# Second attention of a two-block layer: values as the stationary operand, two groups side by side, three branches in one PSUM sum; two more places for expert weights

## Chip, cores, metric

One core of a Trainium2 chip runs the whole program as one launch. The metric is the device time of an execution in microseconds (us). Engines work in parallel, each through its own queue in a fixed order: TensorE (PE; its weight loads are PEld), VectorE (DVE), ScalarE (ACT), GpSimd (POOL) and SyncE (SP), which here issues nearly all weight loads.

## What is computed

Two transformer blocks on 256 tokens of width 1024, fp32 throughout. The first has a forgetting attention beside a convolution, a cross attention to a memory, and a hierarchical mixture of 32 experts. The second has an HGRN2 mixer beside a sparse attention, then a feed-forward part and a gated embedding. The change is in the sparse attention and in the places for expert weights. With 256 tokens the 16 selectable blocks and the window of 512 hold all causal keys, so "selected" and "window" are two causal attentions with keys and values of their own, over the same rotated queries:

```python
s = einsum('bgrqd,bgnd->bgrqn', qb, k_cmp); p_cmp = masked_softmax(s, cmp_end <= t)   # 15 compressed keys
o_cmp = einsum('bgrqn,bgnd->bgrqd', p_cmp, v_cmp)
o_sel = einsum('bgrqk,bgqkd->bgrqd', masked_softmax(qr @ kg, m_sel), vg)              # causal
o_win = einsum('bgrqk,bgkd->bgrqd', masked_softmax(qr @ kwb, m_win), vwb)             # causal
out = gt[:, :, 0] * o_cmp + gt[:, :, 1] * o_sel + gt[:, :, 2] * o_win                 # 16 heads, 4 groups g of 4 heads r, d = 64
merged = sigmoid(ga) * (y_a @ w_branch_a) + sigmoid(gb) * (y_b @ w_branch_b)          # y_b = out
```

## The kernel before

Dense products split fp32 into two fp32r parts (activations into h and l, weights into wh by ScalarE, L184, and wl by VectorE, L185) and add three products in PSUM. `dense_nat` takes 512 output columns at a time: 48 matmuls per call, two loads of 1 MB into the `ring` of four places, each split in two pieces. Instructions are put in order for each engine by a planner that simulates the program and takes, of what is ready, that with the highest priority; `high_priority(offset=n)` moves a part ahead by n instructions. Weight loads and splits are 1000 ahead, the second attention (`att`) is `ATT` = 1300 ahead of its place, so dense products fill in where attention isn't ready.

Expert weights come in loads of 1 MB (one expert's half matrix) into "places" that open as memory of the first block comes free: 8 (`NRB`) when the first attention is done, the four of the ring, 2 + 2 + 2 more, three pairs of the split buffers, and 1 (`NRD`) at the end of the cross attention. `mload` fills place after place in turn; the first 22 loads need nothing of the routing.

In the second block `nsa` makes compressed keys and values and the compressed branch (L1448 to L1480: P is turned, multiplied with the block-diagonal VB and copied into yb), then keys (kh, kl, both halves of the partitions hold a copy), values vt and rotated queries qr (one half of the partitions the h part, the other the l part). Then `att` runs head by head: scores of both branches at once (for queries 0 to 127 against 128 keys, for queries 128 to 255 against 256), the largest of each row by VectorE, exponentials with their sums by ScalarE, three transposes of P per branch, and P times V with P as the stationary operand and 64 columns of vt moving. For each pair of heads VectorE scales the sums out of PSUM and adds both branches to yb. Beside it run the rest of `gate("a")`, `gate("b")` and the product with w_branch_a. After it yb is turned by 16 transposes into the operand of w_branch_b. Tiles of 4 KB per partition (qr, kh, kl, yb, the second gate, ...) share 16 slots (`s4`).

Of the kernel before, what the change touches and what calls it, by code (L numbers as in the profile page):

```python
# [8 lines left out]
F32 = mybir.dt.float32  # L9
# [3 lines left out]
OP = mybir.AluOpType  # L13
# [4 lines left out]
D = 1024  # L18
# [11 lines left out]
NRB, NR2, NRC, NRE, NRD = 8, 2, 2, 2, 1  # L30
# [107 lines left out]
class B:  # L138
# [25 lines left out]
    def wload(self, ap, kc, n, ring=None):  # L164
# [25 lines left out]
    def wchunk(self, ap, kc, n, ring=None):  # L190
        with self.tc.high_priority(offset=self.ahead):
            return self.wsplit(self.wload(ap, kc, n, ring), kc, n)
# [4 lines left out]
    def dense_nat(self, xT, w, K, c0, n, evac, halves=2, ring=None):  # L197
# [4 lines left out]
        for kg in range(0, KC, 4):  # L202
            g = min(4, KC - kg)
            wh, wl = self.wchunk(w[kg * 128:(kg + g) * 128, c0:c0 + n], g, n, ring)
# [935 lines left out]
    def mixer(self, on):  # L1140
# [4 lines left out]
        with tc.tile_pool(name="sm2", bufs=1) as self.sm, tc.tile_pool(name="b2", bufs=1) as b2, \  # L1145
# [21 lines left out]
            with tc.tile_pool(name="hg", bufs=2) as hg:  # L1167
                yb, att = self.hgrn(uT, W, on, hv, hg, php, self.nsa(uT, W, s4, b2))
            self.tap("on", ya[0])
            first.close()  # L1170
            with tc.tile_pool(name="s5", bufs=2) as s5p, tc.tile_pool(name="ap", bufs=1) as ap, \
# [4 lines left out]
                with tc.high_priority(offset=ATT):  # L1176
                    att(ap, pax)
# [27 lines left out]
                self.tap("yb0", yb[0])  # L1205
                self.tap("yb1", yb[1])
                yT = self.tr_parts(yb, self.parts(s4p, tag="s4"))

# [7 lines left out]
                for c in range(2):  # L1216
                    self.dense_nat(yT, A["w_branch_b_2"], D, c * 512, 512, ev_m(c))
# [133 lines left out]
    def nsa(self, uT, W, s4, b2):  # L1351
# [15 lines left out]
        VB = b2.tile([64, 4, 64], F32, name="VB")  # L1367
        nc.gpsimd.memset(KB, 0.0)

        def compress():  # L1370
# [36 lines left out]
            for c in range(2):  # L1407
# [4 lines left out]
            V.tensor_tensor(VB, pk[:, 1, None, :].to_broadcast([64, 4, 64]),  # L1412
                            self.cst("blk")[:64, :, None].to_broadcast([64, 4, 64]), op=OP.mult)
# [32 lines left out]
        yb = [s4("yb") for _ in range(2)]  # L1446

        for hf in range(2):  # L1448
# [68 lines left out]
        def att(ap, pax):  # L1517

            acc, Ps, PTs = {}, {}, {}

            def scores(h):
                g, j = h // 4, h % 2
                if not j:
                    acc[h // 2] = (self.pat.tile([128, 2, 2, 2, 64], F32, name="po"),
                                   self.sm.tile([128, 2, 2, 2], F32, name="asm", bufs=3))
                sm = acc[h // 2][1]
                nm = self.sm.tile([128, 2, 2], F32, name="anm", bufs=2)
                P = Ps[h] = ap.tile([128, 2, 384], F32, name="P", bufs=2)  # L1530
                rr = slice(64 * j, 64 * j + 64)
                for hf, kb, c0 in ((0, 128, 0), (1, 256, 128)):
                    sc = self.ptr.tile([128, 2, kb], F32, name="tr")
                    q = qr[g][:, h % 4, hf * 128:(hf + 1) * 128]
                    self.mm(sc, q, kh[g // 2][:, g % 2, :, :kb], True, False)
                    self.mm(sc, q[rr], kl[g // 2][rr, g % 2, :, :kb], False, False)
                    self.mm(sc[:, :, kb - 128:], self.idr,
                            self.cnr[:, None, :].to_broadcast([128, 2, 128]), False, True)
                    self.exps(sc, P[:, :, c0:c0 + kb], kb, nm[:, hf, :], sm[:, hf, :, j])

            def turn(h):
                P = Ps.pop(h)
                PT = PTs[h] = ap.tile([128, 2, 384], F32, name="PT", bufs=2)
                for br in range(2):
                    pt = pax.tile([128, 384], F32, name="hp")
                    for b in range(3):
                        nc.tensor.transpose(pt[:, b * 128:(b + 1) * 128], P[:, br, b * 128:(b + 1) * 128], idn)  # L1547
                    (V.tensor_copy if br else nc.scalar.copy)(PT[:, br, :], pt)

            def values(h):  # L1550
                g, j = h // 4, h % 2
                po, sm = acc[h // 2]
                PT = PTs.pop(h)
                for br in range(2):
                    v = lambda m: vv[br][:, m, g * 64:(g + 1) * 64]
                    self.mm(po[:, 0, br, j, :], PT[:, br, 0:128], v(0), True, True)
                    self.mm(po[:, 1, br, j, :], PT[:, br, 128:256], v(0), True, False)
                    self.mm(po[:, 1, br, j, :], PT[:, br, 256:384], v(1), False, True)
                if not j:
                    return  # L1560
                rc = self.sm.tile([128, 2, 2, 2], F32, name="arc", bufs=2)
                V.reciprocal(rc, sm)
                V.tensor_tensor(rc, rc, gn[:, :, 1:3, h - 1:h + 1], op=OP.mult)
                tt = self.sm.tile([128, 2, 2, 128], F32, name="att", bufs=2)
                V.tensor_tensor(tt.rearrange("p a b (j d) -> p (a b j) d", j=2), po.rearrange("p a b j d -> p (a b j) d"),
                                rc.rearrange("p a b j -> p (a b j)")[:, :, None].to_broadcast([128, 8, 64]), op=OP.mult)
                for hf in range(2):
                    y = yb[hf][:, (h - 1) * 64:(h + 1) * 64]
                    for br in range(2):
                        V.tensor_tensor(y, y, tt[:, hf, br], op=OP.add)  # L1570

            for h in range(18):
                if h < 16:
                    scores(h)
                if 0 < h <= 16:
                    turn(h - 1)
                if h > 1:
                    values(h - 2)
        return yb, att

    def ffn(self, e):
        tc, nc, A = self.tc, self.nc, self.A
# [127 lines left out]
```

## Time and profile before

| | us |
|---|---|
| median of 3 runs | 1335.99 (1333.78 to 1336.66) |
| the profiled execution | 1335.2 |
| its span | 1333.4 |
| TensorE busy in the span | 1222.0 |
| VectorE, ScalarE, GpSimd busy | 609.2, 482.4, 130.0 |
| granted TensorE clock, share of full speed | 0.971 |

A row of instructions gives line, engine, operation, tiles written and read, shapes and count, then the busy time in us and the mean of one in ns. A timeline row gives the start in us, the time in us, and how many instructions are merged in it. An fp32 matmul stands as two passes, one fp32r matmul or transpose as one. Matmuls are pipelined: the end of one lies behind the start of the next.

### The profile page before, as it was taken

How to read it: one execution, taken by the hardware profiler on the slowest of the kernel's cores; microseconds unless marked ns; L12 is line 12 of the kernel's file. 1: busy time of each engine (PE TensorE's matmuls, PEld its weight loads, DVE VectorE, ACT ScalarE, POOL GpSimd, SP SyncE). 2: the span in 40 equal slices, each digit the busy share in tenths (PEclk: the TensorE clock that was granted, in tenths of full speed). 3: DMA queues.
4: the chain of work that ended last, by engine and by line, in shares of the span. 5: the costliest groups of instructions: out<-in, count | busy, mean ns of one | idle time of the engine just before them, and what ended most of it. 6: DMA issues, size and time to landing. Idle time of an engine off the chain costs nothing.

```text
span 1333.4 us, 17835 instructions
## 1 busy us (share of the span) xinstructions
PE 1222.0 (92%) x7122; PEld 882.0 (66%) x7122; DVE 609.2 (46%) x1031; ACT 482.4 (36%) x916; POOL 130.0 (10%) x171
## 2 busy tenths in 40 slices
PE   8889999989978788796968999999999999999997
PEld 7779888844432323141414998888777878989886
DVE  5897655510100000010004677767656667564665
ACT  5676644300000000000004542345655446454553
POOL 3877000000000000000000000015000000000000
PEclk8999999989999898998989999999999999999999
DMA  8333595769999999999998444633521336555551
GB/s 282 127 127 127 199 379 196 299 249 417 421 417 420 419 417 420 417 420 418 417 407 309 159 158 127 204 129 105 179 95 64 105 132 213 184 196 178 202 190 48
DMA packets 106744, 332.38 MB, mean 249 GB/s; under 512 B 6368, under 2 KB 20512, under 8 KB 86176
## 3 DMA queue, kind: packets, MB, share of 16 engines
q1 hardware_dynamic: 106096, 329.87, 65.7%
q10 hardware_dynamic: 560, 1.31, 0.4%
q8 instruction: 58, 0.95, 0.3%
q14 instruction: 30, 0.25, 0.1%
HBM read 330.11 MB, written 1.05 MB: 248 GB/s over the span
## 4 chain that ended last, share of the span: by engine, by line
PE 48%; DMA 28%; ACT 1%; DVE 1%; issue 0%; DVEq 0%; POOLq 0%; SPq 0%; ACTq 0%
PE mm L195 29%; DMA w<-w_up_in 8%; DMA w<-w_down_in 8%; DMA w<-w_gate_in 7%; PE z L195 7%; PE bg L195 3%; DMA wh<-w_up_in 3%; PE po L195 2%; PE hp L195 2%; PE tr L195 2%; DMA wh<-w_gate_in 1%; PE sp L195 1%; PE hp L1547 1%; DMA w<-w_in_in 0%; ACT wh L184 0%
## 5 line engine op out<-in xcount | busy, mean ns | idle before, releaser
L185 DVE TENSOR_TENSOR wl<-w,wh 128x1024 fp32r<-128x1024 f32 (+2 forms) x228 | 278.9, 1238 | 158.6 <-ACT wh L184 157.4
L184 ACT CAST wh<-w 128x1024 fp32r<-128x1024 f32 (+2 forms) x228 | 235.6, 1044 | 201.7 <-PE mm L195 154.0
L195 PE MATMUL bg<-w,xs 128*32 128x512 f32 x888 | 172.9, 668 | 60.7 <-DMA w<-w_up_in 36.4
L195 PE MATMUL mm<-xTh,wl 128*128 128x256 f32 x688 | 195.6, 289 | 11.1 <-DVE wl L185 11.1
L195 PE MATMUL mm<-xTh,wh 128*128 128x256 f32 x688 | 190.2, 289 | 5.3 <-ACT wh L184 2.8
L195 PE MATMUL mm<-xTl,wh 128*128 128x256 f32 x688 | 193.3, 287 | 0.2 <-DVE xTl L253 0.2
L195 PE MATMUL mm<-wl,xTh 128*128 128x512 f32 (+1 forms) x440 | 173.1, 396 | 0.3 <-DVE wl L185 0.3
L195 PE MATMUL mm<-wh,xTh 128*128 128x512 f32 (+1 forms) x440 | 168.4, 401 | 4.3 <-ACT wh L184 1.3
L195 PE MATMUL mm<-wh,xTl 128*128 128x512 f32 (+1 forms) x440 | 170.3, 394 | 0.0
L195 PEld LDWEIGHTS bg<-w,xs 128*32 128x32 f32 x888 | 38.2, 119 | 179.5 <-issue 77.9
L195 PEld LDWEIGHTS mm<-xTh,wl 128*128 128x128 f32 x688 | 132.5, 193 | 14.1 <-DVE wl L185 13.5
L195 PEld LDWEIGHTS mm<-xTh,wh 128*128 128x128 f32 x688 | 129.6, 193 | 7.9 <-ACT wh L184 3.3
L195 PEld LDWEIGHTS mm<-xTl,wh 128*128 128x128 f32 x688 | 131.8, 193 | 0.8 <-DVE xTl L253 0.4
L988 DVE SCALAR_TENSOR_TENSOR sg<-bg,rsl,sg 128x512 f32<-128x512 f32 x8 | 6.0, 751 | 254.9 <-PE bg L195 254.9
L195 PEld LDWEIGHTS mm<-wh,xTh 128*128 128x128 f32 x440 | 82.4, 189 | 21.9 <-ACT wh L184 1.8
L195 PEld LDWEIGHTS mm<-wl,xTh 128*128 128x128 f32 x440 | 83.1, 189 | 18.0 <-DVE wl L185 1.9
L195 PEld LDWEIGHTS mm<-wh,xTl 128*128 128x128 f32 x440 | 83.0, 189 | 17.8 <-issue 0.7
L195 PE MATMUL bg<-w,ht 128*32 128x512 f32 x456 | 80.0, 598 | 3.5 <-DMA w<-w_down_in 2.8
L195 PEld LDWEIGHTS sp<-oh,X 128*128 128x128 f32 x256 | 61.5, 328 | 12.7 <-issue 10.9
L195 PE MATMUL sp<-oh,X 128*128 128x128 f32 x256 | 65.0, 403 | 0.0
L463 POOL TENSOR_TENSOR zc<-zc,zt 128x256 f32<-128x256 f32 x60 | 63.1, 1052 | 17.3 <-ACT zt L460 12.6
L996 ACT COPY ht<-sp 128x512 f32<-128x512 f32 x8 | 4.7, 586 | 139.8 <-PE sp L994 139.8
(414 smaller groups left out, 1538.2 us busy)
## 6 DMA issues: line engine op xcount, KB each, us to landing
w<-w_down_in SPq DMA_DIRECT2D x73, 1024.0 KB, 16.2
w<-w_up_in SPq DMA_DIRECT2D x68, 1024.0 KB, 15.0
w<-w_gate_in SPq DMA_DIRECT2D x59, 1024.0 KB, 19.9
w<-w_in_in SPq DMA_DIRECT2D x41, 1024.0 KB, 5.3
w<-w_mkv_in SPq DMA_DIRECT2D x8, 1024.0 KB, 5.0
w<-w_out_in SPq DMA_DIRECT2D x8, 1024.0 KB, 5.1
wh<-w_up_in SPq DMA_DIRECT2D x12, 512.0 KB, 17.5
wl<-w_up_in SPq DMA_DIRECT2D x12, 512.0 KB, 13.9
```

Of the source, the lines that this page charges most:

```text
L184: self.nc.scalar.copy(hv, raw[:, j:j + g, :])
L185: self.nc.vector.tensor_tensor(lv, raw[:, j:j + g, :], hv.bitcast(F32), op=OP.subtract)
L195: return self.nc.tensor.matmul(out, lhsT, rhs, start=start, stop=stop, skip_group_check=True)
L463: nc.gpsimd.tensor_tensor(zi, zi, t, op=OP.add)
L988: V.scalar_tensor_tensor(sg, ps, rsl[q], sg, op0=OP.mult, op1=OP.mult)
L996: nc.scalar.copy(ht, tp)
L1547: nc.tensor.transpose(pt[:, b * 128:(b + 1) * 128], P[:, br, b * 128:(b + 1) * 128], idn)
```

## The change

`NRB` goes from 8 to 9 and `NRD` from 1 to 2; the memory reserved for descriptors made on GpSimd shrinks (`dynamic_dma_scratch_size=1024`). Attention goes by steps of one half of the queries, one pair of groups G, one head r, one group gi of the pair. The product of q with kl runs over all 128 rows. P is scaled by gate and sum before it is turned. The P of four heads and two groups is gathered in PT, and then values are the stationary operand: 64 columns of vt for each of two groups, on the two halves of the output's partitions, with 512 columns of PT moving; the compressed branch is added in the same PSUM sum. The sum is split into h and l and is already the operand of w_branch_b; its weight rows are loaded in a matching order, as two DMAs of 64 partitions.

```diff
-NRB, NR2, NRC, NRE, NRD = 8, 2, 2, 2, 1
+NRB, NR2, NRC, NRE, NRD = 9, 2, 2, 2, 2
...
+        if pairs:                                                      # in wload
+            for i in range(2):
+                r = slice(64 * i, 64 * i + 64)
+                self.loaded = self.nc.sync.dma_start(
+                    v[r], ap[kc * r.start:kc * r.stop].rearrange("(k p) n -> p k n", p=64))
+            return v
...
                 with tc.high_priority(offset=ATT):
-                    att(ap, pax)
+                    yb = self.parts(s4p, tag="s4")
+                    att(ap, pax, yb)
...
-                yT = self.tr_parts(yb, self.parts(s4p, tag="s4"))
...
-                    self.dense_nat(yT, A["w_branch_b_2"], D, c * 512, 512, ev_m(c))
+                    self.dense_nat(yb, A["w_branch_b_2"], D, c * 512, 512, ev_m(c), pairs=True)
...
-        VB = b2.tile([64, 4, 64], F32, name="VB")
+        VB = b2.tile([128, 2, 4, 64], F32, name="VB")
...
-            pt = self.ptr.tile([64, 4, 128], F32, name="tr")
-            for r in range(4):
-                nc.tensor.transpose(pt[:, r, :], P2[:, r].rearrange("p g n -> p (g n)"), idn)
-            PT = self.sm.tile([64, 4, 128], F32, name="cPT")
-            V.tensor_copy(PT, pt)
-            for r2 in range(2):
-                po = self.pat.tile([128, 2, 4, 64], F32, name="po")
-                for r in range(2):
-                    self.mm(po[:, r].rearrange("p g d -> p (g d)"), PT[:, 2 * r2 + r, :],
-                            VB.rearrange("p g d -> p (g d)"), True, True)
-                for r in range(2):
-                    nc.scalar.copy(yb[hf].rearrange("p (g r d) -> p g r d", g=4, r=4)[:, :, 2 * r2 + r, :], po[:, r])
+            pt = self.ptr.tile([128, 2, 128], F32, name="tr")
+            for r in range(2):
+                nc.tensor.transpose(pt[:, r, :], P2[:, 2 * r:2 * r + 2].rearrange("p a g n -> p (a g n)"), idn)
+            cPT.append(b2.tile([128, 2, 128], F32, name=f"cPT{hf}"))
+            V.tensor_copy(cPT[hf], pt)
...
+        def att(ap, pax, out):
+            yh, yl = out
+            Ps, PTs = {}, {}
+            steps = [(hf, G, r, gi) for hf in range(2) for G in range(2) for r in range(4) for gi in range(2)]
+
+            def scores(n):
+                hf, G, r, gi = steps[n]
+                kb = 128 * (hf + 1)
+                sm = self.sm.tile([128, 2], F32, name="asm", bufs=3)
+                nm = self.sm.tile([128, 2], F32, name="anm", bufs=3)
+                P = Ps[n] = ap.tile([128, 2, 256], F32, name="P", bufs=3)[:, :, :kb]
+                sc = self.ptr.tile([128, 2, kb], F32, name="tr")
+                q = qr[2 * G + gi][:, r, hf * 128:(hf + 1) * 128]
+                self.mm(sc, q, kh[G][:, gi, :, :kb], True, False)
+                self.mm(sc, q, kl[G][:, gi, :, :kb], False, False)
+                self.mm(sc[:, :, kb - 128:], self.idr, self.cnr[:, None, :].to_broadcast([128, 2, 128]), False, True)
+                self.exps(sc, P, kb, nm, sm)
+                V.reciprocal(sm, sm)
+                h = 4 * (2 * G + gi) + r
+                for br in range(2):
+                    V.tensor_scalar(P[:, br, :], P[:, br, :], sm[:, br:br + 1], gn[:, hf, 1 + br, h:h + 1],
+                                    op0=OP.mult, op1=OP.mult)
+
+            def turn(n):
+                hf, G, r, gi = steps[n]
+                P = Ps.pop(n)
+                if not r and not gi:
+                    PTs[hf, G] = ap.tile([128, 2, 2, 2, 4, 128], F32, name="PT", bufs=2)
+                pt = pax.tile([128, 2, hf + 1, 128], F32, name="hp")
+                for br in range(2):
+                    for m in range(hf + 1):
+                        nc.tensor.transpose(pt[:, br, m, :], P[:, br, m * 128:(m + 1) * 128], idn)
+                (V.tensor_copy if gi else nc.scalar.copy)(PTs[hf, G][:, :, :hf + 1, gi, r, :], pt)
+
+            def values(hf, G):
+                PT = PTs.pop((hf, G))
+                po = self.pat.tile([128, 4, 128], F32, name="po")
+                rows = [slice(64 * gi, 64 * gi + 64) for gi in range(2)]
+                for a in range(2):
+                    for gi in range(2):
+                        self.mm(po[rows[gi], a::2, :], VB[:, a, 2 * G + gi, :], cPT[hf], not a, False)
+                for br in range(2):
+                    for m in range(hf + 1):
+                        for gi in range(2):
+                            g = 2 * G + gi
+                            self.mm(po[rows[gi]], vv[br][:, m, g * 64:(g + 1) * 64], PT[:, br, m, gi], False,
+                                    br == 1 and m == hf)
+                t = slice(hf * 128, (hf + 1) * 128)
+                self.split_out(po, yh(4 * G, 4)[:, :, t], yl(4 * G, 4)[:, :, t])
+
+            for n in range(len(steps) + 2):
+                if n < len(steps):
+                    scores(n)
+                if 0 < n <= len(steps):
+                    turn(n - 1)
+                if n > 1 and (n - 1) % 8 == 0:
+                    values(*steps[n - 2][:2])
...
-    nc = bacc.Bacc("TRN2", target_bir_lowering=False, num_devices=1)
+    nc = bacc.Bacc("TRN2", target_bir_lowering=False, num_devices=1, dynamic_dma_scratch_size=1024)
```

The code that goes from `att` is in the functions printed above (L1517 to L1579).

## Rows read from the trace of the kernel before

**Rows 1.** The page: busy us (share of the span) xinstructions of each engine

```profile
PE 1222.0 (92%) x7122; PEld 882.0 (66%) x7122; DVE 609.2 (46%) x1031; ACT 482.4 (36%) x916; POOL 130.0 (10%) x171
```

**Rows 2.** Windows: stretch, length, each engine's busy us, granted clock, DMA share, GB/s

```profile
264.00:278.00 14.00, 14.00 (x79) 9.98 (x82) 4.38 (x21) 1.80 (x4) 0.00 (x0) 1.00 0.02 8
300.00:700.00 400.00, 332.22 (x1711) 124.36 (x1711) 24.68 (x47) 15.61 (x28) 0.99 (x2) 0.95 1.02 417
880.00:953.00 73.00, 72.52 (x367) 59.26 (x366) 52.09 (x81) 38.33 (x64) 25.13 (x54) 1.00 0.40 130
953.00:1066.00 113.00, 113.00 (x633) 90.02 (x632) 66.73 (x134) 60.78 (x175) 0.00 (x0) 1.00 0.29 95
```

**Rows 3.** Timeline of SyncE's queue: start, us, loads into expert places

```profile
255.94 0.44 SPq L868 DMA_DIRECT2D wh<-w_down_in  x1
278.45 0.80 SPq L868 DMA_DIRECT2D w<-w_down_in  x2
```

**Rows 4.** Timeline of TensorE inside the attention: start, us, instructions

```profile
988.20 0.40 PE L195 MATMUL mm<-wl,xTh 128*128 128x512 f32 x1
988.43 0.39 PE L195 MATMUL mm<-wh,xTl 128*128 128x512 f32 x1
988.66 0.38 PE L1547 MATMUL hp<-cs,P 128*128 128x128 f32 x2
988.79 0.48 PE L195 MATMUL tr<-kh,qr 128*128 128x512 f32 x1
989.20 0.50 PE L195 MATMUL tr<-kl,qr 64*128 64x512 f32 x1
989.63 0.39 PE L195 MATMUL tr<-cnr,idr 128*128 128x256 f32 x1
989.85 0.49 PE L1547 MATMUL hp<-cs,P 128*128 128x128 f32 x3
990.18 0.78 PE L195 MATMUL po<-vt,PT 128*128 128x64 f32 x6
990.77 0.36 PE L195 MATMUL tr<-kh,qr 128*128 128x256 f32 x1
991.07 0.38 PE L195 MATMUL tr<-kl,qr 64*128 64x256 f32 x1
991.38 0.38 PE L195 MATMUL tr<-cnr,idr 128*128 128x256 f32 x1
991.60 0.40 PE L195 MATMUL mm<-wh,xTh 128*128 128x512 f32 x1
```

**Rows 5.** Timeline of TensorE in a dense product of 256 columns

```profile
762.00 0.28 PE L195 MATMUL mm<-xTh,wh 128*128 128x256 f32 x1
762.12 0.28 PE L195 MATMUL mm<-xTh,wl 128*128 128x256 f32 x1
```

**Rows 6.** Timeline of TensorE: compression, two tiles of 64 columns side by side

```profile
834.65 2.16 PE L195 MATMUL po<-w,xc 128*64 128x256 f32 x18
```

**Rows 7.** Timeline of TensorE: an expert's product, four tiles side by side (two rows each)

```profile
302.48 0.60 PE L195 MATMUL bg<-w,ht 128*32 128x512 f32 x2
302.91 0.60 PE L195 MATMUL bg<-w,ht 128*32 128x512 f32 x2
```

**Rows 8.** Timeline of TensorE: the compressed branch, one of four groups

```profile
892.02 1.13 PE L195 MATMUL po<-VB,cPT 64*128 64x256 f32 x4
893.08 0.50 PE L195 MATMUL mm<-wh,xTl 128*128 128x512 f32 x1
```

**Rows 9.** VectorE by line and shape: busy us, mean ns of one, idle before

```profile
L1570 DVE TENSOR_TENSOR yb<-yb,att 128x128 f32<-128x128 f32 x32 | 7.6, 279 | 0.0
L1565 DVE TENSOR_TENSOR att<-po,arc 128x512 f32<-128x512 f32 x8 | 5.5, 686 | 1.0 <-PE po L195 1.0
L1258 DVE TENSOR_SCALAR fo<-fo,lm,lb 128x256 f32<-128x256 f32 x8 | 3.0, 417 | 0.0
L1562 DVE RECIPROCAL arc<-asm 128x8 f32<-128x8 f32 x8 | 1.6, 199 | 0.7 <-ACT P L324 0.6
```

More of the change, by code (lines that the diff above doesn't have):

```diff
@@ L161, in bcast, with wload @@
         return bass.AP(tensor=ap.tensor, offset=ap.offset, ap=[[0, 128], [1, n]])
-    def wload(self, ap, kc, n, ring=None):
+    def wload(self, ap, kc, n, ring=None, pairs=False):
         t = ring.tile([128, 2048], F32, name="w") if ring else self.ring.tile([128, self.RW], F32, name="w")
         v = t[:, :kc * n].rearrange("p (k n) -> p k n", k=kc)
+        if pairs:
[4 more added lines that the diff above has]
+            return v
         self.loaded = self.nc.sync.dma_start(v, ap.rearrange("(k p) n -> p k n", p=128))
@@ L188, in wsplit, with wchunk, dense_nat @@
         return hs, ls
-    def wchunk(self, ap, kc, n, ring=None):
+    def wchunk(self, ap, kc, n, ring=None, pairs=False):
         with self.tc.high_priority(offset=self.ahead):
-            return self.wsplit(self.wload(ap, kc, n, ring), kc, n)
+            return self.wsplit(self.wload(ap, kc, n, ring, pairs), kc, n)
     def mm(self, out, lhsT, rhs, start, stop):
         return self.nc.tensor.matmul(out, lhsT, rhs, start=start, stop=stop, skip_group_check=True)
-    def dense_nat(self, xT, w, K, c0, n, evac, halves=2, ring=None):
+    def dense_nat(self, xT, w, K, c0, n, evac, halves=2, ring=None, pairs=False):
         xh, xl = xT
@@ L203, in dense_nat @@
             g = min(4, KC - kg)
-            wh, wl = self.wchunk(w[kg * 128:(kg + g) * 128, c0:c0 + n], g, n, ring)
+            wh, wl = self.wchunk(w[kg * 128:(kg + g) * 128, c0:c0 + n], g, n, ring, pairs)
             for h in range(halves):
@@ L1167, in mixer @@
             with tc.tile_pool(name="hg", bufs=2) as hg:
-                yb, att = self.hgrn(uT, W, on, hv, hg, php, self.nsa(uT, W, s4, b2))
+                att = self.hgrn(uT, W, on, hv, hg, php, self.nsa(uT, W, s4, b2))
             self.tap("on", ya[0])
@@ L1366, in nsa @@
         KB = b2.tile([128, 4, 30], F32, name="KB")
-        VB = b2.tile([64, 4, 64], F32, name="VB")
+        VB = b2.tile([128, 2, 4, 64], F32, name="VB")
         nc.gpsimd.memset(KB, 0.0)
+        nc.gpsimd.memset(VB, 0.0)
         def compress():
@@ L1411, in compress @@
             V.tensor_scalar(KB[64:128, :, 15:30], k, 0.5, None, op0=OP.mult)
[L1412 to L1413 removed]
+            for a in range(2):
+                V.tensor_tensor(VB[64 * a:64 * a + 64, a], pk[:, 1, None, :].to_broadcast([64, 4, 64]),
+                                self.cst("blk")[:64, :, None].to_broadcast([64, 4, 64]), op=OP.mult)
         qT = [s4("qT", [128, 4, S]) for _ in range(2)]
@@ L1445, in nsa @@
         V.tensor_scalar(gn.rearrange("p h b n -> p h (b n)"), ps, 0.5, 0.5, op0=OP.mult, op1=OP.add)
-        yb = [s4("yb") for _ in range(2)]
+        cPT = []
         for hf in range(2):
@@ L1515, in nsa @@
                 V.tensor_tensor(d[q], ps[r], d[r].bitcast(F32), op=OP.subtract)
[L1517 to L1543, printed above, removed]
-                for br in range(2):
[L1545 to L1553, printed above, removed]
-                for br in range(2):
[L1555 to L1578, printed above, removed]
@@ L1579, in nsa @@
-        return yb, att
+        def att(ap, pax, out):
[16 more added lines that the diff above has]
+                h = 4 * (2 * G + gi) + r
+                for br in range(2):
+                    V.tensor_scalar(P[:, br, :], P[:, br, :], sm[:, br:br + 1], gn[:, hf, 1 + br, h:h + 1],
[6 more added lines that the diff above has]
+                pt = pax.tile([128, 2, hf + 1, 128], F32, name="hp")
+                for br in range(2):
+                    for m in range(hf + 1):
[5 more added lines that the diff above has]
+                rows = [slice(64 * gi, 64 * gi + 64) for gi in range(2)]
+                for a in range(2):
+                    for gi in range(2):
[15 more added lines that the diff above has]
+                    values(*steps[n - 2][:2])
@@ L1581, in ffn @@
+        return att
     def ffn(self, e):
```

2 lines of the change are left out of this document (removed).

## Prediction

> **What bounds the kernel now.** Read the busy times first: TensorE works 92% of the span, no other engine half of it [rows 1]. So a saving counts only where TensorE, or the weight stream, ends last. The table of windows tells which it is where. From 300 to 700 us (the experts) TensorE is busy 332 of 400 us and the DMA share is 1.02 at 417 GB/s: the weights bound. In 880 to 953 (compressed branch, keys, queries) and 953 to 1066 (the attention inside dense products) TensorE has 72.5 of 73 and 113.0 of 113 us, VectorE 71% and 59%, the DMA share is 0.40 and 0.29: TensorE bounds [rows 2]. There a matmul costs the distance from its start to the next start, not its listed duration, since neighbours overlap. The timeline of one head gives these distances [rows 4].
>
> **Two more expert places.** The last load into a place goes out at 255.94 us; the next waits until 278.45, when the first place is used up [rows 3]. In between the queue is empty: 8 GB/s from 264 to 278 [rows 2]. Two more places of 1 MB (1.049 million bytes) fit there; from 280 on the stream is full to its end, so each load taken from it saves 1.049/0.417 = 2.5 us: **-5.0 us**. It would be 0 if the ninth or the second late place came free only after 278; I take the full 5, since 14 idle us hold over five loads. The scratch size goes with it: no descriptor of this path is made on GpSimd when no token overflows, so it only frees memory.
>
> **The wide score product.** A score tile has three products. For the second half of the queries (512 columns) their distances are 0.41 (988.79 to 989.20), 0.43 and 0.22 us; for the first half (256 columns) 0.30, 0.31 and 0.22 [rows 4]. A plain product of the same type takes 0.23 us for 512 columns (988.20 to 988.43) [rows 4] and 0.12 for 256 [rows 5]. The middle product uses 64 rows of the array, its neighbours 128, and all three pay. With 128 rows throughout I expect 0.23+0.23+0.12 = 0.58 and 3 x 0.12 = 0.36: 1.06-0.58 = 0.48 and 0.83-0.36 = 0.47 saved, 16 tiles of each: 15.2. In some tiles the first distance was shorter already, so I take **-14.8 us**. Bounds: 0, if the distances belong to these tiles and not to the change of row count, and 15.2.
> TensorE: Matmul & The Clock Gate, section "Why this matters for your kernels", in the Trainium skill says that a product over 32 rows takes the time of one over 128. By that alone widening gives 0 here. TensorEngine Tiling (Array Packing), "Key Properties", in the same skill, says that changing the tiling mode drains the array; by that the gain is the full one. The rows side with the second: 0.43 against 0.23 us for equal columns [rows 4].
>
> **Values stationary.** Gone are 96 products, each fp32 and so two passes, of 64 columns: six passes take 0.59 us (990.18 to 990.77), 192 take 18.9 [rows 4]. Gone too are 8 compressed products in four groups of 1.06 us (892.02 to 893.08) [rows 8], 4.2, and about 0.1 on entering each. In their place come 24 products of 512 columns and 16 of 256, 80 passes, in pairs on two halves of the array's columns. Two such tiles side by side are in this trace: 18 passes of 256 columns in 2.16 us, each 0.38 long, so nine rounds 0.22 apart [rows 6]. For 512 columns the expert products (four tiles side by side) give 0.43 per round (302.48 to 302.91) [rows 7]. So 24 x 0.43 + 16 x 0.22 = 13.8, and 0.3 for each of four entries and exits (estimate: the 0.2 that a change adds on each side of the middle product [rows 4], less what overlaps): 15.0. Net 18.9 + 4.2 + 0.4 - 15.0 = **-8.5 us**. Bounds: +5.3 if the two tiles don't overlap (13.8 more), -9.7 without entries.
>
> **Transposes.** 16 of yb go, and 4 of the compressed P; three take 0.33 us (989.85 to 990.18) [rows 4], so 20 x 0.11 = **-2.2 us**. The 96 of P stay, in other groups. TensorE's sum: -14.8 - 8.5 - 2.2 = **-25.5 us**, 5 of it before 953.
>
> **What VectorE and ScalarE pay.** Gone: 32 additions into yb (7.6 us), 8 scalings out of PSUM (5.5), 8 reciprocals and as many small products (1.6, and about as much) [rows 9]: 16. New: 32 reciprocals of two columns, and 64 scalings of P by two column scalars, half of 128 columns, half of 256. The nearest scaling with two scalars is 417 ns for 256 columns; the reciprocal of 8 columns 199 [rows 9]. I take 0.40 and 0.25 (half the columns, not half the time) and 0.15: 12.8 + 8.0 + 4.8 = 25.6, bounds 20 and 31 (all at 417 ns and 0.13). Net +10, so VectorE has 66.7 + 10 = 77 us in a stretch of which TensorE's work is 113 - 20.5 = 92.5. ScalarE keeps its 61 us [rows 2]: the exponentials and the PSUM copies keep their columns (8 copies into yb go, before 953). The new waits are the reciprocals': each waits for ScalarE's exponentials, and behind it in VectorE's queue stand the next reduction and the weight splits, for which TensorE's dense products wait. So attention's steps now lean on VectorE (83%), where before there was slack. TensorE's cover is the dense work in between: 221 of the 633 products of the stretch (633 less 96 score, 96 transposes of P, 192 value passes, 28 other transposes), 51 us. It is not free to lie anywhere: the new yb takes four of 16 slots before the second gate asks for its two, and these come free when queries and keys of the first two groups have been read, at step 24 of 32; where this order leaves attention alone, a step waits for VectorE. From below the loss is 0. From above: VectorE at the 71% that it had in 880 to 953 beside a full TensorE [rows 2] needs 77/0.71 = 108 us, 16 lost. I take **+6**, nearer the lower end, since TensorE never waits in this stretch now.
>
> **The rest.** The weights of the second branch come in two halves of 64 partitions, four DMAs more. They are asked during the attention with the DMA share at 0.29 [rows 2] and the ring four loads deep: 0; each would cost some us if the ring ran dry. The split of yb's sum (4 + 4 instructions) only moves. VB's second half is one more small VectorE instruction, the narrower cPT copies less. No wait stands in front of SP's queue that was not there.
>
> **Sum.** The profiled execution took 1335.2 us (span 1333.4), 0.8 below the median of the runs shown. 1335.2 - 5.0 - 25.5 + 6 = 1310.7; on the median 1311.5, say **1311**.
>
> **Rivals.**
> *Nothing is lost.* VectorE keeps up at 83%: 1311 - 6 = 1305. For it: TensorE without a gap at 71% [rows 2]. Against: each step now has VectorE twice in its chain, before and after the exponentials.
> *VectorE bounds the attention.* 16 lost instead of 6: 1321. For it: the computed share; against: weight splits can be done ahead. TensorEngine Tiling (Array Packing), section "PSUM Bottleneck", in the Trainium skill warns of this: tiling speeds up TensorE and not the way out of PSUM. Here the way out keeps its size and softmax grows, so by that rule it is this rival; no run here shows it yet.
> *The narrow product was not the cause:* the scores keep their distances, 1311 + 14.8 = 1326. The rows speak against it.
> *The places bring nothing:* 1316.
> *Slower: attention cut off from its filler.* Place: the slots for the second gate. If attention keeps its old pace, 113/32 = 3.5 us a step [rows 2], through 24 steps, with only the rest of the first gate and half of the second beside it (about 23 us of dense), these take 84 us; the last 8 steps (17 us of TensorE) and the remaining 30 us of dense follow: 131, 18 more than before. With 5 from the earlier stretch and 5 from the experts: 1336 + 18 - 10 = 1344. It decides from (113 + 10 - 47)/24 = 3.2 us a step. Against it: 3.5 is with dense products beside every step.
>
> **How the numbers follow.** Forecast (1308 to 1314) 0.42; nothing lost 0.25; VectorE 0.15; no gain of the scores 0.05; places 0.05; slower 0.06; 0.02 that it cancels out. What a measurement of this kernel can't tell from no change is about 0.2% (2.7 us). Faster 0.91, same 0.02, slower 0.07. Range 1301 to 1324: it holds forecast, nothing lost, VectorE and the places with 3 or 4 us for the prices in between.
>
> **What would show it.** The middle score product with 128 rows, and distances of 0.23 and 0.12 us; value passes in pairs with one start, 0.43 apart; no L1570; from 278 on the same 417 GB/s, and the last expert load 5 us earlier. Counted from the end of the experts, the second branch's first product would come about 19 us earlier. Wrong would be: value passes one after the other; score distances as now; TensorE gaps ended by VectorE or ScalarE of more than 10 us in the attention; a weight load of the second branch as a releaser.

## The result, and the profile after

The changed kernel takes 1318.86 us (median of 4 runs, 1318.28 to 1320.46) beside 1336.22 for the kernel before (1333.78 to 1336.66 in 4 runs): ratio 0.9876, interval 0.9859 to 0.9893, 17.4 us less. The profiled execution took 1318.28 us with a span of 1316.6, 16.9 us less than before. The forecast was 1311, so 8 us of the forecast gain are missing.

The page of the changed kernel, the line of busy times that answers to [rows 1], and below it the windows that answer to [rows 2]: the pause in the weight stream, the experts, the compressed branch up to the attention's first score, and the attention up to its last value pass.

```profile
PE 1196.2 (91%) x6974; PEld 859.7 (65%) x6974; DVE 619.1 (47%) x1072; ACT 479.3 (36%) x908; POOL 131.1 (10%) x172
```

```profile
264.00:278.00 14.00, 14.00 (x77) 10.06 (x80) 4.38 (x21) 1.80 (x4) 0.00 (x0) 1.00 0.18 73
300.00:700.00 400.00, 326.53 (x1726) 124.39 (x1726) 25.16 (x47) 16.19 (x29) 0.00 (x0) 0.93 1.02 417
865.00:938.00 73.00, 70.31 (x379) 59.10 (x379) 55.28 (x91) 35.92 (x55) 26.51 (x55) 1.00 0.42 136
938.00:1044.00 106.00, 103.14 (x519) 74.20 (x518) 76.96 (x173) 63.16 (x179) 0.00 (x0) 1.00 0.39 106
```

Two things differ from [rows 2]. The window of the attention is 106 us long instead of 113 (the one before runs 2 us beyond its last value pass; from the first score product to the instruction behind the last value pass it is 105 instead of 110), and VectorE is busy 77.0 us in it, the 77 of the forecast. But TensorE now has 2.7 us without work in the 73 us ahead of the attention and 2.9 inside it, where it had 0.5 and none.

SyncE's queue, answering to [rows 3], sends three loads from 255.75 us on where it sent one; the next refill is still at 278.70. The last load of an expert lands at 708.3 us; before it was 713.1.

```profile
255.75 0.87 SPq L875 DMA_DIRECT2D w<-w_down_in  x2
256.68 0.42 SPq L875 DMA_DIRECT2D wh<-w_down_in  x1
278.70 0.81 SPq L875 DMA_DIRECT2D w<-w_gate_in  x2
```

One score tile of 512 columns, answering to [rows 4]: the distances are 0.31 (behind transposes), 0.23 and 0.11 us, where they were 0.41, 0.43 and 0.22.

```profile
1019.72 0.60 PE L1553 MATMUL hp<-cs,P 128*128 128x128 f32 x4
1020.08 0.48 PE L202 MATMUL tr<-kh,qr 128*128 128x512 f32 x1
1020.39 0.39 PE L202 MATMUL tr<-kl,qr 128*128 128x512 f32 x1
1020.62 0.28 PE L202 MATMUL tr<-cnr,idr 128*128 128x256 f32 x1
1020.73 0.40 PE L202 MATMUL mm<-wh,xTl 128*128 128x512 f32 x1
```

The value passes of one sum (queries 128 to 255, first pair of groups) stand in two pieces: two passes that cost 1.00 us (1004.82 to 1005.82), other work, then 14 passes in 3.58 us (1007.42 to 1011.00).

```profile
1004.82 1.07 PE L202 MATMUL po<-PT,vt 128*64 128x512 f32 x2
1005.82 1.09 PE L305 MATMUL mm<-cs,on 128*128 128x128 f32 x8
...
1007.42 3.65 PE L202 MATMUL po<-PT,vt 128*64 128x512 f32 x14
1011.00 0.33 PE L1553 MATMUL hp<-cs,P 128*128 128x128 f32 x1
```

The waits of TensorE, by what ended them (total, times, longest), first in the 73 us ahead of the attention, then inside it:

```profile
PE mm L202 <- DVE sgt L320: 1.5, 1, 1.5
PE mm L202 <- DVE wl L192: 0.8, 1, 0.8
PE hp L202 <- ACT A L1334: 0.5, 1, 0.5
...
PE tr L202 <- ACT P L331: 1.7, 2, 1.2
PE po L202 <- DVE asm L1539: 0.8, 1, 0.8
```

This view leaves out the part of a wait that falls under the modelled end of the matmul before it. Counted from start to start, over the median distance of the same instruction, the waits of more than 0.25 us are 3.3 us ahead of the attention (912 to 924) and 3.7 inside it (976 to 992), 7.0 together; in the kernel before they are 0.6.

VectorE's new rows, answering to [rows 9] (no addition into yb is left): the scalings of P cost 0.41 and 0.34 us, the reciprocals 0.16.

```profile
L1542 DVE TENSOR_SCALAR P<-P,asm,gn 128x256 f32<-128x256 f32 x32 | 11.7, 408 | 0.3
L1542 DVE TENSOR_SCALAR P<-P,asm,gn 128x128 f32<-128x128 f32 x32 | 9.5, 343 | 0.5
L1539 DVE RECIPROCAL asm<-asm 128x2 f32<-128x2 f32 x32 | 5.1, 158 | 1.9 <-ACT P L331 1.8
```

### The profile page after: what moved, and what is told of

The parts are those of the page before. It is cut to its first block, busy times and chain, and to the rows that moved or that the text cites. A ratio compares the mean times of both kernels' runs of the same rounds, so it can differ in the third digit from the quotient of the medians.

```text
span 1316.6 us, 17594 instructions
## 1 busy us (share of the span) xinstructions
PE 1196.2 (91%) x6974; PEld 859.7 (65%) x6974; DVE 619.1 (47%) x1072; ACT 479.3 (36%) x908; POOL 131.1 (10%) x172
## 4 chain that ended last, share of the span: by engine, by line
PE 48%; DMA 26%; DVE 2%; ACT 1%; issue 0%; SPq 0%; DVEq 0%; POOLq 0%; ACTq 0%
PE mm L202 29%; DMA w<-w_up_in 9%; DMA w<-w_gate_in 8%; PE z L202 7%; DMA w<-w_down_in 4%; PE bg L202 4%; PE hp L202 2%; DMA wh<-w_down_in 2%; DMA wl<-w_down_in 2%; PE po L202 2%; PE sp L202 1%; PE tr L202 1%; PE hp L1553 1%; DMA w<-w_in_in 0%; ACT wh L191 0%
## 5 line engine op out<-in xcount | busy, mean ns | idle before, releaser
L202 PE MATMUL bg<-w,xs 128*32 128x512 f32 x1024 | 178.9, 701 | 69.6 <-DMA w<-w_up_in 49.6
L202 PE MATMUL mm<-xTh,wl 128*128 128x256 f32 x688 | 195.7, 289 | 11.1 <-DVE wl L192 11.1
L202 PE MATMUL bg<-w,ht 128*32 128x512 f32 x320 | 69.3, 597 | 2.1 <-DMA w<-w_down_in 1.4
L470 POOL TENSOR_TENSOR zc<-zc,zt 128x256 f32<-128x256 f32 x60 | 63.3, 1055 | 17.0 <-ACT zt L467 12.3
## 6 DMA issues: line engine op xcount, KB each, us to landing
wl<-w_down_in SPq DMA_DIRECT2D x24, 512.0 KB, 13.8
```

Source lines behind the costliest of these rows:

```text
L202: return self.nc.tensor.matmul(out, lhsT, rhs, start=start, stop=stop, skip_group_check=True)
L470: nc.gpsimd.tensor_tensor(zi, zi, t, op=OP.add)
```

## Experiments

Two things that no edit here aimed at move the times. The last expert pass starts at 706.9 to 710.1 us in kernels with the two more places. And in the traced execution of six kernels (the runs named places, narrow, pairs first, serial, dead products, all in one piece) some 41 us behind the second branch TensorE runs about 3 us at the lower of its two clocks, which costs 1.5 us; the last section shows it. So beside each median stands the length of **the stretch**: from the start of the last expert pass to the first transposes behind the second branch (TensorE's timeline; in the changed kernel 708.8 to 1063.7). It holds all parts of the change but the places. It comes from one traced execution each; kernels that hold the same instructions in it agree to 0.4 us (before and e1, e2 and e9, changed and e4). In e10 it holds 14 dense products fewer than in e7, so that row can't be compared as it stands.

| kernel | median us | ratio, interval | stretch us |
|---|---|---|---|
| before | 1336.2 | 1 | 366.8 |
| changed | 1318.9 | 0.9876 (0.9859 to 0.9893) | 354.9 |
| e1 places alone | 1331.1 | 0.9963 (0.9951 to 0.9976) | 366.5 |
| e2 wide product alone | 1323.1 | 0.9901 (0.9881 to 0.9921) | 354.5 |
| e9 places and wide product | 1318.1 | 0.9864 (0.9844 to 0.9884) | 354.1 |
| e3 changed, narrow product | 1333.7 | 0.9980 (0.9969 to 0.9991) | 367.8 |
| e4 changed, sums later | 1317.5 | 0.9858 (0.9838 to 0.9879) | 354.9 |
| e5 changed, pairs first | 1321.4 | 0.9882 (0.9863 to 0.9902) | 357.1 |
| e6 changed, no scaling | 1317.0 | 0.9865 (0.9846 to 0.9885) | 353.0 |
| e7 changed, joint copies | 1313.8 | 0.9837 (0.9816 to 0.9858) | 351.5 |
| e8 changed, serial tiles | 1327.6 | 0.9937 (0.9920 to 0.9955) | 363.1 |
| e10 joint, own memory | 1316.4 | 0.9854 (0.9829 to 0.9880) | 349.7 (less work in it) |
| e11 changed, dead products | 1322.5 | 0.9892 (0.9875 to 0.9909) | 357.1 |
| e12 joint, all in one piece | 1316.1 | 0.9845 (0.9828 to 0.9862) | 349.5 |

**e1, the places alone.**

```diff
-NRB, NR2, NRC, NRE, NRD = 8, 2, 2, 2, 1        # on the kernel before, with the scratch size
+NRB, NR2, NRC, NRE, NRD = 9, 2, 2, 2, 2
```

> The kernel before with nothing changed but the two more places for expert weights (NRB 9, NRD 2, and the smaller descriptor memory that makes room for them). Theory (the stream of expert weights bounds from 280 us on, and each load that goes out in the empty stretch before 278 saves 2.5 us): 5.0 us faster, ratio 0.9963, the last expert load lands about 4.8 us earlier as it did in the changed kernel. Rival (the stages behind the experts swallow it): no change, ratio 1.000.

Measured: 0.9963, so 4.9 us of 1336, with the stretch unchanged (366.5). The theory holds; nothing behind the experts swallows it. In the traced execution the last load lands at 706.5 us, 6.6 ahead of the kernel before (in the changed kernel 4.8), and 1.5 us are lost again to the lower clock behind the second branch.

**e2, the wide score product alone.**

```diff
-                    self.mm(sc, q[rr], kl[g // 2][rr, g % 2, :, :kb], False, False)   # kernel before
+                    self.mm(sc, q, kl[g // 2][:, g % 2, :, :kb], False, False)
```

> The kernel before with one edit: the product of q with kl runs over all 128 rows, which adds a product of the parts' remainders. Theory (the change of the row count between neighbouring products costs about 0.2 us on each side): the distances of kl and cnr fall to 0.23 and 0.12 us, about 12 us less on TensorE (11 to 15), ratio 0.991 (0.989 to 0.992), TensorE still without gaps. Rival (the distances belong to these tiles, whatever the rows): distances as before and ratio 1.000. Second rival (TensorE shrinks, but VectorE and ScalarE then end the steps): distances fall and gaps of several us appear, ratio 0.995.

Measured: 13.3 us less, the stretch 12.3 less. TensorE's timeline of this kernel, one tile of 512 columns as in [rows 4]:

```profile
991.67 0.38 PE L1547 MATMUL hp<-cs,P 128*128 128x128 f32 x2
991.81 0.48 PE L195 MATMUL tr<-kh,qr 128*128 128x512 f32 x1
992.12 0.39 PE L195 MATMUL tr<-kl,qr 128*128 128x512 f32 x1
992.35 0.28 PE L195 MATMUL tr<-cnr,idr 128*128 128x256 f32 x1
992.47 0.49 PE L1547 MATMUL hp<-cs,P 128*128 128x128 f32 x3
```

0.31, 0.23, 0.12: with equal rows throughout, the added work costs nothing and the changes of row count go. What stays is the 0.31 of the first product. Behind a dense product it is 0.23 in the changed kernel; behind transposes or value passes 0.08 more. With the narrow product behind it (e3) the same two are 0.33 and 0.41. So 0.08 of the 0.41 were never due to the row count. That is most of the forecast's error in this term: 0.08 on 24 of 32 tiles, 1.9 of 2.5 us.

**e3, the narrow product put back into the changed kernel.**

```diff
-                self.mm(sc, q, kl[G][:, gi, :, :kb], False, False)
+                self.mm(sc, q[64 * (r % 2):64 * (r % 2) + 64], kl[G][64 * (r % 2):64 * (r % 2) + 64, gi, :, :kb], False, False)
```

> The changed kernel with one edit taken back: the product of q with kl runs over 64 rows again (32 of them, the row half by the head's parity as before). Theory: distances of 0.4 and 0.3 us come back, 11 to 13 us more on TensorE; of these some 3 us vanish in the gaps in which TensorE waits for VectorE and ScalarE, so 8 to 12 us slower than the changed kernel, ratio to the kernel before 0.994 to 0.997. Rival (the score products were never it): as the changed kernel, 0.9876.

Measured: 14.9 us slower than the changed kernel, 12.9 of it in the stretch. The timeline shows the old distances, 0.41, 0.43, 0.22:

```profile
1021.99 0.48 PE L202 MATMUL tr<-kh,qr 128*128 128x512 f32 x1
1022.40 0.50 PE L202 MATMUL tr<-kl,qr 64*128 64x512 f32 x1
1022.83 0.39 PE L202 MATMUL tr<-cnr,idr 128*128 128x256 f32 x1
1023.05 0.60 PE L1553 MATMUL hp<-cs,P 128*128 128x128 f32 x4
```

The 12.9 are not the score products alone. In this traced execution TensorE ran at the lower clock (0.50) from 986.5 to 993.3 us, inside the attention, where the changed kernel had 1.00; 2.3 us of distance beyond the medians fall in there. Without distances of more than 0.25 us over their median the score products cost 12.0 us more than in the changed kernel. I expected that the waits would take 3 us of it up; outside that spell those of the attention fell from 3.7 to 2.2 us, so they took up 1.5.

**e9, the two parts together, without the rest of the change.** Both edits above on the kernel before.

> The kernel before with the two parts that were run alone put together: the two more expert places and the product of q with kl over 128 rows; the attention is as before otherwise (P as the stationary operand, yb turned at the end). What the changed kernel has beyond this one is the values stationary, with all that goes with it. Theory of the forecast (this part saves 8.5 and 2.2 us of TensorE and pays 6 in waits): this kernel is 4 to 5 us slower than the changed one, ratio to the kernel before 0.991. Rival (the traces: 6.3 us saved on TensorE, 6.3 us of new waits, so the part brings nothing): as fast as the changed kernel, 0.986 to 0.988, which is also the sum of the two parts run alone.

Measured: 1318.1, the stretch 354.1 beside 354.9. The rival holds: **the values stationary, with all that goes with them, bring nothing** that these runs can tell (ratios 0.9864 and 0.9876, each within about 0.002). TensorE's starts, summed by kind of instruction over the stretch of both kernels, say why. From this kernel to the changed one the value passes fall from 19.5 to 14.9 us, the transposes of yb from 1.5 to 0, those of the compressed P by 0.3, the compressed products from 4.2 to 4.1: 6.6 saved. The waits grow from 0.6 us (between 865 and 1064) to 7.0: 6.3 paid. The stretch is even 0.8 longer: two more dense products (0.5 us) lie ahead of its end, and small rises make up the rest. In this kernel the view of waits has for the same 200 us a single row:

```profile
PE mm L195 <- DVE sgt L313: 0.5, 1, 0.5
```

**e8, the column tiles one after the other**, to see whether a pair is worth a pass.

```diff
-                for br in range(2):
-                    for m in range(hf + 1):
-                        for gi in range(2):
+                for gi in range(2):
+                    for br in range(2):
+                        for m in range(hf + 1):
```

> The changed kernel with all value passes of the one group issued ahead of those of the other, so that the two column tiles do not overlap. Theory (a round of two passes side by side costs 0.43 us, as one pass alone does): 16 rounds of two become 32 passes alone, 6.9 us slower than the changed kernel, ratio to the kernel before 0.9925 to 0.993. Rival (two passes side by side cost nearly as much as one after the other): below 2 us slower, 0.989.

Measured: value passes 21.9 us instead of 14.9, 7.0 more, and the stretch 8.2 longer. One sum's second group alone:

```profile
1048.08 0.39 PE L202 MATMUL mm<-wh,xTl 128*128 128x512 f32 x1
1048.40 3.65 PE L202 MATMUL po<-PT,vt 128*64 128x512 f32 x8
1051.98 0.50 PE L202 MATMUL mm<-wh,xTh 128*128 128x512 f32 x1
```

Eight passes in 3.58 us: a pass alone costs the 0.43 us of a pair. So pairs do overlap, and each pass of the changed kernel that runs alone wastes its other half.

**e4, the sums one step later.**

```diff
-                if n > 1 and (n - 1) % 8 == 0:
-                    values(*steps[n - 2][:2])
+                if n > 2 and (n - 2) % 8 == 0:
+                    values(*steps[n - 3][:2])
```

> The changed kernel with the value products of a half and pair of groups emitted one step later, so that all copies of P turned are done when they start. Theory (each of the four sums is torn in three groups, and passes run alone because the copy of one group is ready before that of the other): all passes in pairs, 0.43 us apart, four lone passes and two entries fewer per sum: 3.5 to 6 us faster than the changed kernel, ratio to the kernel before 0.983 to 0.985. Rival (the tearing lies in time in which TensorE would wait anyway, or the last sum, now a step later, stands before the second branch): no change, 0.9876, or 1 us worse.

Measured: nothing, and for a plain reason: the planner put all instructions in the same order as in the changed kernel, since it takes what is ready and not what is written next. It tells nothing of the theory; it is a second measurement of the changed kernel (1317.5).

**e7, joint copies.** A tile of turned P now holds both groups, and one instruction copies it. Since two P wait for one copy, P has four buffers instead of three. An excerpt; the comment is not in the code:

```diff
...
+                for br in range(2):                                     # second half of the queries
+                    pt = pax.tile([128, 2, 2, 128], F32, name="hp")
+                    for m in range(2):
+                        for gi in range(2):
+                            nc.tensor.transpose(pt[:, m, gi, :], Pk[gi][:, br, m * 128:(m + 1) * 128], idn)
+                    (V.tensor_copy if br else nc.scalar.copy)(PT[:, br, :, :, r, :], pt)
...
```

> The changed kernel with the turned P of both groups in one PSUM tile, copied by one instruction, so that both column tiles of the value products become ready at the same moment. Theory (16 of the 48 value passes run alone, because one group's copy is ready before the other's): all passes go in pairs 0.43 us apart, eight rounds fewer, and an entry or two less per sum: 3 to 5 us faster than the changed kernel, ratio to the kernel before 0.984 to 0.985. Rival (the lone passes lie in time in which TensorE would wait anyway, or the joint copy makes the steps wait longer): 0.9876 or above.

Measured: 1313.8, the stretch 3.4 shorter than in the changed kernel, and value passes of 11.1 us instead of 14.9 (compressed passes of 4.8 instead of 4.1). This is the fastest kernel of the study, 1.6% below the one before. The last sum in one piece:

```profile
1034.95 0.39 PE L202 MATMUL mm<-wh,xTh 128*128 128x512 f32 x1
1035.27 3.65 PE L202 MATMUL po<-PT,vt 128*64 128x512 f32 x16
1038.86 0.50 PE L202 MATMUL mm<-wl,xTh 128*128 128x512 f32 x1
```

16 passes in 3.59 us, eight rounds, where the changed kernel pays 1.00 + 3.58 for as many. There ScalarE's copy of one group is ready first, the planner sends that group's first matmul ahead alone, and that tile stays one matmul ahead to the end: four passes of each sum, 16 of 48, have no partner.

**e6, no scaling.** The 64 scalings and 32 reciprocals of L1539 to L1543 are taken out; the two branches stay unnormalised and ungated.

> The changed kernel without the 32 reciprocals and 64 scalings of P by gate and sum on VectorE: the selected and the window branch are left unnormalised and ungated. Theory of the VectorE chain (the scalings, some 25 us of VectorE, are what the steps wait for): the waits of TensorE between 973 and 994 us (3.7 us) are gone, 3 to 4 us gained, ratio 0.985. Rival (what lacks is a dense product beside the steps): with a chain shorter by some 0.9 us a step half of the waits stay, 1 to 2 us gained, 0.9865. If VectorE bound the attention as a whole (the rival of the prediction) it would be 10 us or more.

Measured: 1317.0; the waits inside the attention fall from 3.7 to 1.8 us (waits over 0.25 us), the stretch by 1.9. That is the half that the rival gave. VectorE doesn't bound the attention as a whole, 25 us less of it give 2. Where the steps run without dense products beside them, its work stands in their chain. The chain of waits of the changed kernel at 975 to 980 us (start, us, what) shows it:

```profile
975.24 0.42 DVE anm L327
975.67 0.60 DVE xTl L258
...
977.03 0.60 DVE P L1542 x2
977.64 0.11 DVE asm L1539
977.77 0.60 DVE P L1542 x2
978.38 0.67 DVE anm L327 x2
979.09 0.24 issue
979.33 0.56 ACT P L331 x3
```

**e5, pairs of groups first**, so that queries and keys of the first pair are read after 16 steps.

```diff
-            steps = [(hf, G, r, gi) for hf in range(2) for G in range(2) for r in range(4) for gi in range(2)]
+            steps = [(hf, G, r, gi) for G in range(2) for hf in range(2) for r in range(4) for gi in range(2)]
```

> The changed kernel with the steps of the attention in another order: both halves of the queries of the first pair of groups, then both of the second, so that the queries and keys of the first pair are done after 16 steps instead of 24 and their slots go to the second gate earlier. Theory (the 3.7 us in which TensorE waits between 973 and 994 us come from steps without a dense product beside them, because the second gate had no slot): the gate's first product comes some 10 us earlier and 2 to 4 us are gained, ratio to the kernel before 0.985 to 0.986. Rival (the steps' chain through VectorE and ScalarE sets the pace, whatever stands beside it): the waits only move, 0.9876.

Measured: 2.2 us longer in the stretch, waits of 4.7 us. The theory of an earlier gate fails as it was put: ScalarE evacuates the second gate's first product at 1007.3 us, behind step 29, not 10 us earlier but 14 later (993.4 in the changed kernel), though the slots that its tiles take over had been read at step 15. What keeps it back in the planner's order is open.

**e10, memory of its own for the second gate**, on e7.

```diff
-                gate("b", 7728, s4)
+                gate("b", 7728, lambda name: ap.tile([128, D], F32, name=name, bufs=1, tag=f"sgb{next(own)}"))
...
-                    PTs[hf, G] = ap.tile([128, 2, 2, 2, 4, 128], F32, name="PT", bufs=2)
+                    PTs[hf, G] = [ap.tile([128, 2, 2, 4, 128], F32, name="PT", bufs=3) for br in range(2)]
```

> The kernel with the joint copies, with memory of its own for the second gate's two tiles (turned P kept per branch in three places of 8 KB instead of two of 16 makes room for it), so that the gate waits for no slot of queries or keys. The first evacuation of the gate then stands behind step 8 of the attention in ScalarE's order instead of step 21, and its second half of products lies beside the attention earlier. Theory of the slots: of the 3.5 us of waits of TensorE between 970 and 990 us 2 to 3 are gone, 1 to 3 us faster than the kernel with the joint copies, ratio to the kernel before 0.982. Rival (with the filler used up earlier the waits come later in the attention instead): as the kernel with the joint copies, 0.9837.

The edit also copies the turned P of the first half by branch, two copies where e7 has one.

Measured: the order is as the theory has it. ScalarE evacuates the second gate's first product behind 8 of the 32 score tiles (964.2 us); in the changed kernel and in e7 this came behind 23 (993.4 and 988.8 us), in e9 behind 7 (965.5). The waits that the view lists for TensorE from 930 to 1065 us fall from 2.4 us in e7 to 1.1. But the time doesn't follow: the median is 2.7 us above that of e7, with intervals that overlap. The stretch, 1.8 us shorter, misleads here: 14 dense products that e7 has in it come behind its end, 3.2 us at 0.23 each. For equal work it is 1.4 longer, and the lower clock that TensorE had from 989.6 us on for about 3 us lies in it. From its end to the end of the program it is 257.8 us instead of 252.9: the moved products, and results of the second branch that come at a bad moment (a wait of 1.1 us of the transposes for VectorE, 1.0 of the products behind them for ScalarE). So the slots did hold the filler back; that freeing them gains time is not shown.

**e11, dead products** in the place of the compressed ones that had gone.

```diff
             V.tensor_copy(cPT[hf], pt)
+            for r2 in range(2):
+                po = self.pat.tile([128, 2, 4, 64], F32, name="po")
+                for r in range(2):
+                    self.mm(po[:, r].rearrange("p g d -> p (g d)"), cPT[hf][:, r2, :],
+                            VB[:, r].rearrange("p g d -> p (g d)"), True, True)
```

> The changed kernel with eight products of 256 columns put back in the compressed branch (turned P by VB, as the kernel before had them, but over 128 rows); nothing reads their sums. In the traces the changed kernel lost its cover there: TensorE waits 3.3 us between 912 and 924 us for VectorE and ScalarE, where the kernel before waited 0.6. Theory (the 4.2 us of compressed products that went from this stretch were cover, so taking them away gained next to nothing): the 16 passes, some 3.5 us, fit into the waits: 0 to 1 us slower than the changed kernel, ratio to the kernel before 0.9876 to 0.9885, waits in the stretch down to 1 us or less. Rival (TensorE's work counts in full here too): 3.5 us slower, 0.990.

Measured: the 16 passes cost 3.1 us, the waits there fall from 3.3 to 1.1 (one row is left below), and the stretch grows by 2.2. So neither: part of the removed work had been cover, but more of it counted than I expected. That the waits of 912 to 924 came with the moved work is shown; that the move gained nothing is not.

```profile
PE mm L202 <- DVE sgt L320: 1.0, 1, 1.0
```

**e12, compressed passes behind the value passes**, on e7: the loop over VB moves below the loop over vt, with the start flag on the first value pass and the stop flag on the last compressed one.

> The kernel with the joint copies, with the compressed passes put behind the value passes in each sum, so that all passes of a sum stand in one piece. Theory (each entry into the two column tiles and each exit costs 0.26 to 0.31 us, and the sums are entered 8 to 12 times): four entries and exits fewer, 2 us faster than the kernel with the joint copies, ratio to the kernel before 0.982. Rival (the order around it moves and the waits with it): 0.983 to 0.985, no difference that can be told.

Measured: the stretch is 2.0 us shorter, the 2 of the theory, but not by its price alone: from the starts the passes of both kinds fall by 1.3 us, from 15.8 to 14.5, and 0.8 of that are the compressed passes of the last sum, in three pieces in e7 and in one here. The median is 2.3 above that of e7, and the intervals overlap. The last expert load landed 2.4 us later in its profile (709.6 against 707.2) and the slow 3 us behind the second branch cost 1.5. Whether it is the better kernel isn't settled.

## Why the prediction came out 8 us low

Its terms, beside what the runs measured for each:

| term | forecast | measured | from |
|---|---|---|---|
| places | -5.0 | -4.9 | e1 |
| wide score product | -14.8 | -12.3 | stretch of e2 |
| values stationary | -8.5 | -4.8 | starts, e9 to changed |
| transposes | -2.2 | -1.8 | starts, e9 to changed |
| waits | +6 | +6.3 | starts, e9 to changed |
| sum | -24.5 | -17.5 | profiles: -16.9 |

**The mechanisms were right, two sizes were not.** *Scores:* "The rows side with the second", and they did, in both directions: 12.3 us less in e2 and 12.0 more in e3 for 32 tiles. The size forgot that a first product behind transposes or value passes keeps 0.08 us that were never due to the row count. The Trainium skill says in TensorEngine Tiling (Array Packing), "Key Properties", that changing the tiling mode drains the array; e2 and e3 agree with it. *Values:* "24 x 0.43 + 16 x 0.22 = 13.8, and 0.3 for each of four entries and exits" is the step that failed. The price of a round was right (0.43, e7 and e8), yet the value and compressed passes cost 19.0 us, not 15.0. The sum took for granted that every pass finds its partner and each sum stands in one piece. The planner tears each into three (compressed passes, one early matmul, the rest), so 16 passes run alone. Joint copies give back 3.8 us of value passes, and the place of the compressed passes 2.0 in the stretch; with both, value and compressed passes cost 14.5 (e12) instead of 19.0, under the 15.0 of the forecast.

The same page of the Trainium skill, under "When to Use Tiling", recommends the swap of the two operands with column tiling where 64 columns move. Here the passes themselves bear it out: 23.7 us before, 19.0 in the changed kernel, 14.5 at best. What the changed kernel gained by it, it lost in waits.

*Waits:* the size came out right in part by luck, since the place was half wrong. The forecast looked for them in the attention's steps without filler, and 3.7 us are there, with VectorE in the chain (e6) and the second gate held back by its slots to step 23 (e10 shows the order), as it said. The other 3.3 lie ahead of the attention, where the compressed products left; the forecast counted their 4.2 us as saved in full.

**The rivals.** *VectorE bounds the attention* (1321) is nearest by its number, but not by its mechanism: e6 takes 25 us of VectorE away and gains 2. *The narrow product was not the cause* fell with e2, *the places bring nothing* with e1. *Slower* did not come: the steps without filler ran at 1.6 us each (12 steps from 974.6 to 993.7 us), far below the 3.2 from which it would decide.

## What to carry to other kernels

Price a part by the stretch it lies in, and measure parts alone: here two small edits made the whole gain and the large rewrite in the middle cancelled itself out, which the total hid. Column tiles pay only as pairs; let one instruction make both operands ready, or a planner that takes what is ready will run some of them alone, here 16 of 48. Work taken from a bound engine is saved in full only while other work stands ready to fill its place.

## What the runs showed that was not expected

The clock. Behind the second branch TensorE stands still for 2.0 us between the transposes of X and the next product, in every kernel. In the traced execution of six kernels the granted clock then fell to 0.50 (the lower level, 1.2 GHz) within 1.4 us after it had resumed, for about 3 us, and rose again while TensorE worked on; in the others it stayed at 1.00. First the kernel with the pairs first (idle 1103.75 to 1105.79), then the changed kernel (idle 1101.78 to 1103.82); the granted clock is the first number behind POOL's:

```profile
1104.00:1106.00 2.00, 0.21 (x2) 0.24 (x3) 2.00 (x7) 2.00 (x7) 0.00 (x0) 1.00 0.68 183
1106.00:1108.00 2.00, 2.00 (x15) 2.00 (x15) 1.74 (x4) 1.97 (x5) 0.00 (x0) 0.74 0.79 261
1108.00:1110.00 2.00, 2.00 (x11) 2.00 (x11) 0.88 (x4) 1.91 (x6) 0.00 (x0) 0.50 0.58 226
1110.00:1112.00 2.00, 2.00 (x17) 2.00 (x16) 0.53 (x3) 0.00 (x0) 0.00 (x0) 0.90 0.01 3
```

```profile
1104.00:1106.00 2.00, 2.00 (x18) 2.00 (x18) 1.74 (x4) 1.97 (x5) 0.00 (x0) 1.00 0.99 376
1106.00:1108.00 2.00, 2.00 (x19) 2.00 (x18) 0.91 (x4) 1.94 (x6) 0.00 (x0) 1.00 0.11 42
```

From the end of the stretch to the end of the program the six take 254.4 us and the others 252.9, but for e10. The same gap in the same code thus costs 1.5 us or not, and no edit aimed at it. In e10 a gap of 1.3 us inside the attention was followed by the lower clock as well (0.50 from 990 to 992 us), and in e3 waits of 1.3 and 0.3 us were (0.50 from 986.5 to 993.3); in the changed kernel a wait of 1.35 us at 978.5 was not. So differences of 1.5 us between two kernels' totals say little. The stretch says more, if it holds the same work and no such spell.
